# A two-layer recurrent decoder step on one Trainium2 core: side work handed out per half chunk in pieces, sample states by a block-diagonal operand, other first loads and another last root

## The chip, the cores and the metric

The kernel runs on one core of a Trainium2 chip. A core has TensorE (PE, matrix products), VectorE (DVE), ScalarE (ACT) and GpSimd (POOL); SyncE (SP) here only issues DMA transfers. The metric is the device time of one execution in microseconds. The time before is the median of three runs; the predicted time is set beside that median.

## The reference, cut to what matters

All in fp32: a prompt of 256 tokens and 8 samples of 8 tokens each, 320 columns together, pass through two layers. Every layer is one large input projection, three recurrent branches, their projections, gates and an output projection.

```python
def _layer(x, pos0, ...):
    xn = _rmsnorm(x, lp['norm_g'])                      # x: (tokens, 2048)
    proj = xn @ lp['w_in']                              # u, z of three branches; q, k, v; three gates
    ...
    y_s5 = ...                                          # diagonal complex recurrence, GELU, GLU
    y_lru = ...                                         # gated linear recurrence after a conv of 4
    y_ret, n_ret = _retention(q, k, v, r_ret, pos0, lp['ret_gn_g'])
    b_s5 = (y_s5 * silu(z_s5)) @ lp['w_branch_s5']
    b_lru = (y_lru * silu(z_lru)) @ lp['w_branch_lru']
    b_ret = (y_ret * silu(z_ret)) @ lp['w_branch_ret']
    merged = sigmoid(g_s5) * b_s5 + sigmoid(g_lru) * b_lru + sigmoid(g_ret) * b_ret
    return x + merged @ lp['w_out'], ...
def _retention(...):                                    # 8 heads, 128 x 128 states
    r_new = r * g_chunk + einsum('bjhd,bjhe->bhde', kc * zeta, vc)
...
y = _rmsnorm(x, final_norm_g)                           # after the second layer
```

For the samples the line `r_new` gives 8 states of 128x128 for every head, each from 8 tokens. All new states are outputs too.

## The kernel before, in words

All weights pass through one stream. A chunk is 512 KB of weights (4 k-tiles of 128 rows, 256 columns); 624 chunks come by DMA on SP's queue into `raw` (4 buffers), in an order written out in `blocks`. Each chunk is used in two half chunks, 1248 in all. For a half chunk ACT writes a rounded copy `whi` of the weights (`copy`, line 126) and DVE the rest `wlo` = raw − whi (`sub`, line 99), both 128x512; then PE runs 12 main matmuls with 320 columns: 2 column halves n, 2 k-tiles kk, 3 passes (lines 1321 to 1323: hi·xh, hi·xl, lo·xh). The activations are split in the same way (`xh`, `xl`; `yhl` for a branch; `GH`; `M`). `whi` and `wlo` share a pool of 4 buffers (`phl`), so that the copy for half chunk u waits for PE's line 1322 of half chunk u−4. They are emitted `lead` half chunks ahead of their use: 3 at most places, up to 8 in chunks 25 to 64, where a tile `more` gives five further buffers.

All other work (the recurrences, gates, norms and states) is side work: Python generators that emit a piece, `yield`, and are resumed by `step`. `stream` calls `step` once after each chunk; `yield n` holds a generator back n chunks. `step` lets a generator wait when the modelled load of DVE or ACT is over `BEHIND`, which is 99 and so never. The emitted order is the order on every engine: a side piece between two half chunks stands between two `wlo` on DVE. Results of side matmuls go to four PSUM buffers `ps`, in turn: a matmul that writes a buffer waits for whatever read the buffer's last content.

Retention, the side work that the change rewrites, runs for head pairs m = 0 to 3 of each layer. `ret_qk` turns q and k (`ra` = `ra` + `rsw`, line 99, 128x640); `ret_heads` multiplies them (line 894, `ps<-ra`), masks the scores (`rsc`, `scs`), transposes keys, and normalizes the result into the gate `z` (`z<-ps,pv,z`) which becomes `yhl`; `ret_state` makes the states. For the samples' states it multiplies values with a 0/1 mask per sample, so that one 128x512 matmul gives four samples (`rvm<-rkv,sm`, two of 128x512 on DVE, then two matmuls at line 1029, then `r<-r,ps`): 64 such muls and 64 such matmuls in all. A recurrence of S5 runs as a long chain of 128x64 operations on POOL (lines 563 to 566) beside retention.

At the start, `constants` and `more_constants` issue pv, ident, sm, pmask and the second pv on ACT's queue, and `x_load(0)` and the first chunk (two halves) on SP's, in turn. At the end, `finish` takes the inverse root of the summed squares: DVE adds eps, ACT takes Ln and Exp (one table load between them), DVE does one Newton step (`rstd`, three operations), and then 8 tiles `y` of two 128x320 halves are multiplied, 14 halves on DVE and 2 on POOL, each stored by a DMA when both its halves are done.

Of the kernel before, what the change touches and what calls it, by code (L numbers as in the profile page):

```python
# [24 lines left out]
SLOT, BEHIND = 3.26, 99  # L25
# [15 lines left out]
K_ZP, K_ZS, K_GP, K_G2, K_MC, K_VM = 0, 16, 24, 48, 72, 74  # L41
NK = 82


def shape_constants():
# [27 lines left out]
    for t in range(2):  # L73
        sm[:, K_MC + t] = ((p // 16) % 2 == t)
    for b in range(NB):
        sm[:, K_VM + b] = (p % 64 // NS == b)
# [4 lines left out]
class Program:  # L81
    def __init__(self, nc, tc, I, O, gamma8):
# [3 lines left out]
        self.load = dict(dve=0.0, act=0.0)  # L86
        self.table = None
# [6 lines left out]
    def dve(self, o, rate=1.04):  # L94
        self.load['dve'] += 0.065 + rate * 1e-3 * math.prod(o.shape[1:])
# [25 lines left out]
    def act(self, o, a, f, **k):  # L121
        self.load['act'] += 0.08 + 0.92e-3 * math.prod(o.shape[1:])
# [14 lines left out]
    def spawn(self, g, late=0):  # L137
        e = [g, 0, late]
        self.gens.append(e)
        self.gens.sort(key=lambda e: e[2])  # L140
        return e

    def step(self):
        for k in self.load:
            self.load[k] = max(0.0, self.load[k] - SLOT)
        for e in list(self.gens):
# [3 lines left out]
            if max(self.load.values()) > BEHIND:  # L150
                continue
            self.advance(e)

    def advance(self, e):
        try:
            r = next(e[0])
            e[1] = (r or 1) - 1
        except StopIteration:
            self.gens.remove(e)

# [15 lines left out]

    def exp_vec(self, out, x, t):
# [7 lines left out]
        yield  # L185
# [3 lines left out]
        yield  # L189
# [3 lines left out]
        yield  # L193

    def rsqrt_vec(self, out, v, t):
# [3 lines left out]
        for _ in range(3):  # L199
            self.mul(t, out, out)  # L200
            self.stt(t, t, -0.5, v, OP.mult, OP.mult)
            self.stt(out, t, 1.5, out, OP.add, OP.mult)


    def constants(self):
# [4 lines left out]
        nc.scalar.dma_start(self.pv[0], I['pv'][0])  # L210
# [3 lines left out]
        nc.vector.memset(self.fv, 1.0)  # L214

    def more_constants(self):
        nc, I = self.nc, self.I
        self.table_of(AF.Ln)
# [3 lines left out]
        nc.scalar.dma_start(self.ident, I['c_ident'])  # L222
        nc.scalar.dma_start(self.sm, I['c_sm'])
        nc.scalar.dma_start(self.pmask, I['c_pair'])
        for l in range(1, DEPTH):
            nc.scalar.dma_start(self.pv[l], I['pv'][l])
# [66 lines left out]
    def x_group(self, q):  # L293

        for c in range(4):
# [7 lines left out]
            if c % 2:  # L303
# [20 lines left out]
    def s5_setup(self, l):  # L324
        nc, I = self.nc, self.I
        t = self.rt([128, 32, 32], name="s5t")
# [21 lines left out]
        yield  # L348
# [10 lines left out]
        self.stt(h, n, -c3, h, OP.mult, OP.add)  # L359
        self.ts(h, h, 0.5, OP.mult)  # L360
        self.mul(z, h, h)
        yield
# [1077 lines left out]
```

## Time and profile before

| what | value |
|---|---|
| median of three runs (lowest, highest) | 2404.8 us (2404.71, 2404.82) |
| profiled execution, own time | 2406.62 us |
| profiled execution, span | 2404.8 us |
| PE busy | 2360.1 us, 98% |
| DVE busy | 1572.1 us, 65% |
| ACT busy | 1070.8 us, 45% |
| POOL busy | 605.9 us, 25% |
| DMA moved | 413.71 MB, mean 172 GB/s |
| mean granted TensorE clock | 0.995 of full speed |

Busy times are sums over the span. PE is the engine to look at: each microsecond in which it has nothing to do, or runs at its lower clock, is a microsecond of the kernel's time, and the other engines matter where PE waits for them.

### The profile page before, as it was taken

How to read it: one execution, taken by the hardware profiler on the slowest of the kernel's cores; microseconds unless marked ns; L12 is line 12 of the kernel's file. 1: busy time of each engine (PE TensorE's matmuls, PEld its weight loads, DVE VectorE, ACT ScalarE, POOL GpSimd, SP SyncE). 2: the span in 40 equal slices, each digit the busy share in tenths (PEclk: the TensorE clock that was granted, in tenths of full speed). 3: DMA queues.
4: the chain of work that ended last, by engine and by line, in shares of the span. 5: the costliest groups of instructions: out<-in, count | busy, mean ns of one | idle time of the engine just before them, and what ended most of it. 6: DMA issues, size and time to landing. Idle time of an engine off the chain costs nothing.

```text
span 2404.8 us, 44311 instructions
## 1 busy us (share of the span) xinstructions
PE 2360.1 (98%) x16746; PEld 2326.9 (97%) x16746; DVE 1572.1 (65%) x2900; ACT 1070.8 (45%) x1941; POOL 605.9 (25%) x1157
## 2 busy tenths in 40 slices
PE   8999999999999999999999999999999999999997
PEld 8999999889999999999999999999999999999997
DVE  7889466876774756755567665767776656555544
ACT  6655344333343434444555554433333334444443
POOL 2004001999920000300100000699950200000011
PEclk9999999999999999999999999999999999999998
DMA  6655587454654545446656587454555554444553
GB/s 213 220 173 166 159 218 211 126 172 159 193 171 164 168 151 173 152 151 195 201 165 190 162 223 206 147 182 137 168 170 168 178 184 157 149 153 146 158 179 118
DMA packets 153590, 413.71 MB, mean 172 GB/s; under 512 B 18592, under 2 KB 59296, under 8 KB 153120
## 3 DMA queue, kind: packets, MB, share of 16 engines
q1 hardware_dynamic: 152656, 410.58, 54.1%
q8 instruction: 131, 2.15, 0.4%
q14 instruction: 83, 0.68, 0.1%
q10 hardware_dynamic: 720, 0.30, 0.0%
HBM read 373.83 MB, written 31.74 MB: 169 GB/s over the span
## 4 chain that ended last, share of the span: by engine, by line
PE 95%; DVE 3%; DMA 1%; issue 0%; ACT 0%; SPq 0%; ACTq 0%; DVEq 0%
PE pt L1321 30%; PE pt L1323 29%; PE pt L1322 29%; DMA raw<-w_in 1%; PE ps L638 1%; PE ps L757 1%; DVE wlo L99 1%; DVE rvm L99 1%; PE ps L546 1%; PE ps L1029 1%; PE ps L894 0%; PE ps L953 0%; ACT whi L126 0%; DVE yt L99 0%; PE ps L1004 0%
## 5 line engine op out<-in xcount | busy, mean ns | idle before, releaser
L99 DVE TENSOR_TENSOR wlo<-raw,whi 128x512 fp32r<-128x512 f32 x1187 | 845.5, 727 | 758.1 <-ACT whi L126 737.4
L126 ACT ACTIVATE whi<-raw 128x512 fp32r<-128x512 f32 x1187 | 737.7, 629 | 1071.3 <-PE pt L1322 894.2
L1321 PE MATMUL pt<-xh,whi 128*128 128x320 f32 x3320 | 1037.5, 313 | 6.1 <-ACT whi L126 6.1
L1323 PE MATMUL pt<-xh,wlo 128*128 128x320 f32 x3320 | 1029.8, 310 | 7.6 <-DVE wlo L99 7.5
L1322 PE MATMUL pt<-xl,whi 128*128 128x320 f32 x3320 | 1027.6, 310 | 0.0
L1321 PEld LDWEIGHTS pt<-xh,whi 128*128 128x128 f32 x3320 | 625.6, 188 | 11.8 <-ACT whi L126 6.4
L1323 PEld LDWEIGHTS pt<-xh,wlo 128*128 128x128 f32 x3320 | 625.0, 188 | 11.5 <-DVE wlo L99 11.3
L1322 PEld LDWEIGHTS pt<-xl,whi 128*128 128x128 f32 x3320 | 625.4, 188 | 2.8
L1321 PE MATMUL pt<-yhl,whi 128*128 128x320 f32 x756 | 234.7, 310 | 0.0
L1323 PE MATMUL pt<-yhl,wlo 128*128 128x320 f32 x756 | 233.6, 309 | 0.0
L1322 PE MATMUL pt<-yhl,whi 128*128 128x320 f32 x756 | 233.6, 309 | 0.0
L563 POOL TENSOR_TENSOR cs<-H,l2r 128x64 f32<-128x64 f32 x254 | 121.2, 477 | 255.6 <-DVE H L113 235.9
L252 POOL TENSOR_TENSOR acc<-acc,sq 128x320 f32<-128x320 f32 x28 | 25.6, 914 | 586.4 <-ACT sq L126 585.4
L1321 PE MATMUL pt<-M,whi 128*128 128x320 f32 x512 | 158.7, 310 | 0.0
L1323 PE MATMUL pt<-M,wlo 128*128 128x320 f32 x512 | 158.2, 309 | 0.0
L1322 PE MATMUL pt<-M,whi 128*128 128x320 f32 x512 | 158.2, 309 | 0.0
L1321 PEld LDWEIGHTS pt<-yhl,whi 128*128 128x128 f32 x756 | 141.9, 188 | 0.8 <-issue 0.5
L1322 PEld LDWEIGHTS pt<-yhl,whi 128*128 128x128 f32 x756 | 141.9, 188 | 0.0
L1323 PEld LDWEIGHTS pt<-yhl,wlo 128*128 128x128 f32 x756 | 141.9, 188 | 0.0
L565 POOL TENSOR_TENSOR cs<-cs,H 128x64 f32<-128x64 f32 x254 | 132.3, 521 | 0.0
L564 POOL TENSOR_TENSOR cs<-H,l2i 128x64 f32<-128x64 f32 x254 | 123.8, 487 | 0.0
L566 POOL TENSOR_TENSOR H<-cs,cs 128x64 f32<-128x64 f32 x254 | 117.7, 463 | 19.9
(251 smaller groups left out, 2526.5 us busy)
## 6 DMA issues: line engine op xcount, KB each, us to landing
raw<-w_in SPq DMA_DIRECT2D x447, 512.0 KB, 4.4
raw<-w_out SPq DMA_DIRECT2D x64, 512.0 KB, 4.5
raw<-wb_lru SPq DMA_DIRECT2D x32, 512.0 KB, 4.7
raw<-wb_ret SPq DMA_DIRECT2D x32, 512.0 KB, 3.8
raw<-wb_s SPq DMA_DIRECT2D x32, 512.0 KB, 3.6
r<-sret SPq DMA_DIRECT2D x16, 512.0 KB, 8.0
ret_s<-r SPq DMA_DIRECT2D x16, 512.0 KB, 3.0
raw<-w_glu SPq DMA_DIRECT2D x16, 512.0 KB, 3.6
```

Source lines behind the costliest of these rows:

```text
L99: self.nc.vector.tensor_tensor(o, a, b, op=op)
L126: self.nc.scalar.activation(o, a, f, **k)
L252: self.nc.gpsimd.tensor_tensor(self.acc, self.acc, sq, op=OP.add)
L546: self.nc.tensor.matmul(pp[g][:, a * HN:(a + 1) * HN], wst[:, a, g * 128:(g + 1) * 128], ust[:, 2 * a + g], start=True, stop=True, skip_gr ...
L563: g.tensor_tensor(t1, old, lr, op=OP.mult)
L564: g.tensor_tensor(t2, self.swap(old), li, op=OP.mult)
L565: g.tensor_tensor(t1, t1, new, op=OP.add)
L566: g.tensor_tensor(new, t1, t2, op=OP.add)
L638: nc.tensor.matmul(o[q * 32:(q + 1) * 32], w[:, c, m], H[:, q0 + m, c, col:col + HN], start=col == 1 and c == 0, stop=c == 1, tile_positio ...
L1321: nc.tensor.matmul(o, hi[:, kk, cs], xh, start=k == 0, stop=False)
L1322: nc.tensor.matmul(o, hi[:, kk, cs], xl, start=False, stop=False)
L1323: nc.tensor.matmul(o, lo[:, kk, cs], xh, start=False, stop=k == nk - 1)
```

## The change

1. **Handing out.** `step` is called after each half chunk. `yield` holds a generator for two half steps (the chunk of before), the new `yield 0` splits a piece: the generator goes on at once unless it is `paced` and the modelled load is over `BEHIND` = 2.4 us; each half step takes `SLOT` = 1.8 us off that load. Long pieces (`exp_vec`, `s5_setup`, `lru_*`, `ret_heads`, ...) get many `yield 0`. `need` forces steps until a flag of the operand that a main matmul is about to read is set. The deep stretch ends at chunk 58 instead of 68, and side work of the setups starts earlier.
2. **Sample states.** The masks, `rkv` and `rvm` go. Keys and values of the samples are spread fourfold over 256 columns (`parts_of`, 32 ACT copies 128x256), transposed (`rows_of`, 64 transposes 128x128, while 16 transposes of line 918 go), and made hi or lo by partition (`rk4`, `rv4`: 16 ACT copies and 16 DVE operations of 128x512, and 16 `rkz` of 128x256 in place of 128x128). Four ACT copies per head (64 in all) write the values on the blocks of `vbd`, a tile that is zero elsewhere, and two matmuls 128x512 per head (32 in all) give the states.
3. **Start.** x comes in two 128x320 parts, pv and one 128x640 on ACT's queue; the first chunk in four parts on SP's; ident, sm, pmask and the second pv go to SP's queue after chunk 8. Eight matmuls ones·ones of 128x128 run first. The first half chunk is split per k-tile and its matmuls run in the order (n, kk) = (0,0), (1,0), (0,1), (1,1).
4. **Last root.** ACT's `Abs_reciprocal_sqrt` reads the sum directly, beside DVE's eps step; one Newton step; the result `rp` is a PSUM tile, and a copy `rs` in SBUF serves POOL, which multiplies 4 halves instead of 2.

```diff
-SLOT, BEHIND = 3.26, 99
+SLOT, BEHIND = 1.8, 2.4
...
-    def step(self):
+    def step(self, force=False):
         for k in self.load:
             self.load[k] = max(0.0, self.load[k] - SLOT)
         for e in list(self.gens):
             if e[1] > 0:
                 e[1] -= 1
                 continue
-            if max(self.load.values()) > BEHIND:
-                continue
-            self.advance(e)
+            while force or not (e[3] and e[4]) or max(self.load.values()) <= BEHIND:
+                if not self.advance(e):
+                    break
 
     def advance(self, e):
+
         try:
             r = next(e[0])
-            e[1] = (r or 1) - 1
         except StopIteration:
             self.gens.remove(e)
+            return False
+        r = 1 if r is None else r
+        e[1], e[4] = max(0, 2 * r - 1), r == 0
+        return r == 0
+
+    def need(self, *flag):
+        for _ in range(400):
+            if self.flag.get(flag):
+                return
+            self.step(force=True)
...
     def rsqrt_of(self, p):
+
         r = self.pl.tile([128, T], F32, name="rstd", tag="rstd")
-        for _ in self.rsqrt_steps(p, r):
-            pass
-        return r
+        v, t, q = (self.vt([128, T]) for _ in range(3))
+        rp = self.ps()[:, :T]
+        self.act(q, p[:, :T], AF.Abs_reciprocal_sqrt, scale=1.0 / D, bias=self.fv[:, 2, 0:1])
+        self.ts(v, p[:, :T], 1.0 / D, OP.mult, EPS, OP.add)
+        self.mul(t, q, q)
+        self.stt(t, t, -0.5, v, OP.mult, OP.mult)
+        self.stt(rp, t, 1.5, q, OP.add, OP.mult)
+        return r, rp
...
+    def rows_of(self, a):
+        p = self.ps()
+        for n in range(2):
+            for c in range(2):
+                q = slice(c * 128, (c + 1) * 128)
+                self.nc.tensor.transpose(p[:, n * 256 + c * 128:n * 256 + (c + 1) * 128], a[:, n, q], self.ident)
+        return p
...
         for n in range(2):
-            h, x = 2 * m + n, kv[n]
-            for s in range(2):
-                t = self.rt([128, 2, 4, 128], F32R, name="rvm")
-                mask = sm[:, K_VM + 4 * s:K_VM + 4 * s + 4][:, :, None].to_broadcast([128, 4, 128])
-                for i in range(2):
-                    self.mul(t[:, i], x[:, 1 + i][:, None, :].bitcast(F32).to_broadcast([128, 4, 128]), mask)
+            h = 2 * m + n
+            for b in range(4):
+                r = slice(32 * b, 32 * b + 32)
+                self.copy(self.vbd[r, :, b], v4[r, n].bitcast(F32))
+            yield
+            for c in range(2):
+                p = self.ps()
+                nc.tensor.matmul(p, k4[:, n, c * 128:(c + 1) * 128], self.vbd[:, c].rearrange("p b e -> p (b e)"),
+                                 start=True, stop=True)
                 yield
-                p = self.ps()
-                for i in range(2):
-                    nc.tensor.matmul(p, x[:, 0], t[:, i].rearrange("p b e -> p (b e)"), start=i == 0, stop=i == 1)
-                yield
-                rr = r0[n][:, 4 * s:4 * s + 4].rearrange("p b e -> p (b e)")
+                rr = r0[n][:, 4 * c:4 * c + 4].rearrange("p b e -> p (b e)")
                 self.stt(rr, rr, self.g8[h], p, OP.mult, OP.add)
...
-                elif j > 4 and n:
-                    nc.gpsimd.tensor_tensor(y[:, n], y[:, n], r, op=OP.mult)
+                elif j > 2 and n:
+                    nc.gpsimd.tensor_tensor(y[:, n], y[:, n], rs, op=OP.mult)
...
-        deep = (27, 2 * 68)
+        deep = (27, 2 * 58)
```

Three places show what moves. First DVE in retention of layer 0, head pair m = 1, in the kernel before: the work between one chunk's `wlo` pair and the next. `cb1`, `cb2` and `H` are a step of S5 (its input states), `r0` the sample state, `rv` the values.

```order
L99 TENSOR_TENSOR wlo_6414<-raw_6353,whi_6413 128x512
L99 TENSOR_TENSOR cb1_6429<-H_3036,l2r_2399 128x256
L99 TENSOR_TENSOR cb2_6430<-H_3036,l2i_2400 128x256
L99 TENSOR_TENSOR cb1_6429<-cb1_6429,cb2_6430 128x256
L99 TENSOR_TENSOR H_3036<-H_3036,cb1_6429 128x32x8
L99 TENSOR_TENSOR rsw_6392<-rsw_6392,ropr_4415 128x640
L99 TENSOR_TENSOR wlo_6442<-raw_6353,whi_6441 128x512
L99 TENSOR_TENSOR wlo_6458<-raw_6395,whi_6457 128x512
L119 SCALAR_TENSOR_TENSOR r0_5911<-r0_5911,ps_6435 128x512
L99 TENSOR_TENSOR rvm_6474<-rkv_6104,sm_126 128x512 x2
L99 TENSOR_TENSOR ra_6338<-ra_6338,rsw_6392 128x640
L99 TENSOR_TENSOR wlo_6482<-raw_6395,whi_6481 128x512
```

The same place in the changed kernel, m = 1; `rv4` and `rk4` stand elsewhere, `rvm` nowhere, and a piece stands after each half chunk.

```order
L98 TENSOR_TENSOR wlo_6520<-raw_6428,whi_6519 128x512
L98 TENSOR_TENSOR wlo_6553<-raw_6477,whi_6552 128x512
L98 TENSOR_TENSOR rv_6568<-pt_6343,rstd_693 128x640
L118 SCALAR_TENSOR_TENSOR r0_5980<-r0_5980,ps_6514 128x512
L98 TENSOR_TENSOR wlo_6576<-raw_6477,whi_6575 128x512
L118 SCALAR_TENSOR_TENSOR z_5998<-ps_6535,pv0_114,z_5998 128x256
L118 SCALAR_TENSOR_TENSOR z_5998<-ps_6535,pv0_114,z_5998 128x64
L98 TENSOR_TENSOR scs_5304<-ps_6550,rdms_6450 64x4x16
L98 TENSOR_TENSOR wlo_6595<-raw_6516,whi_6594 128x512
```

Where four or five operations stood between one `wlo` and the next, at most three stand here, and behind `wlo_6553` stand `rv_6568` and then `r0_5980`, the reader of `ps_6514`; behind `wlo_6576` stand the two `z_5998`, the readers of `ps_6535`.

PE at that place in the changed kernel. The first row is the last main matmul of a half chunk, whose weights are `whi_6454` and `wlo_6455`; line 1076 transposes, lines 970, 971 and 974 are the score products (894, 895 and 898 before).

```order
L1425 MATMUL pt_6518<-xh_158,wlo_6455 128x320
L1076 MATMUL ps_6535<-ident_603,ron_6333 128x128 x3
L970 MATMUL ps_6544<-ra_6199,ra_6378 128x256
L971 MATMUL ps_6544<-ra_6199,ra_6378 128x128
L970 MATMUL ps_6547<-ra_6199,ra_6378 128x256
L971 MATMUL ps_6547<-ra_6199,ra_6378 128x128
L974 MATMUL ps_6550<-ra_6199,rkd_6539 128x128
L1423 MATMUL pt_6518<-xh_164,whi_6479 128x320
```

`ps_6550` is in the buffer of `ps_6514`, so line 974 waits for `r0_5980` above. `wlo_6553`, which stands ahead of that on DVE, is the part of a half chunk four further on: `whi_6552` and `wlo_6553` take the buffers of `whi_6454` and `wlo_6455`, which PE leaves only at the first row. Twelve main matmuls later line 1108 writes `ps_6571`, in the buffer of `ps_6535`, so it waits for the two `z_5998`, which stand behind `wlo_6576`; that one takes the buffers of the half chunk which PE has just finished. No side matmul of the kernel before stands this close to a reader behind such a `wlo`, apart from those that wait for a rotated key or query.

Last, DVE at the very end, before and then in the changed kernel (`ps` in the last three rows is `rp`).

```order
L99 TENSOR_TENSOR sq<-yt 128x320
L115 TENSOR_SCALAR vt<-ps 128x320
L99 TENSOR_TENSOR vt<-rstd 128x320
L119 SCALAR_TENSOR_TENSOR vt<-vt 128x320
L119 SCALAR_TENSOR_TENSOR rstd<-vt,rstd 128x320
L99 TENSOR_TENSOR yt<-yt,rstd 128x320 x6
L119 SCALAR_TENSOR_TENSOR yt<-yt,pv_112,rstd 128x320 x2
L99 TENSOR_TENSOR yt<-yt,rstd 128x320 x6
```

```order
L98 TENSOR_TENSOR sq<-yt 128x320
L114 TENSOR_SCALAR vt<-ps 128x320
L98 TENSOR_TENSOR vt<-vt 128x320
L118 SCALAR_TENSOR_TENSOR vt<-vt 128x320
L118 SCALAR_TENSOR_TENSOR ps<-vt 128x320
L98 TENSOR_TENSOR yt<-yt,ps 128x320 x6
L118 SCALAR_TENSOR_TENSOR yt<-yt,pv_115,ps 128x320 x2
L98 TENSOR_TENSOR yt<-yt,ps 128x320 x4
```

Two halves move from DVE to POOL, and Newton's last operation and its readers go from an SBUF tile to PSUM.

## Rows read from the trace of the kernel before

**Rows 1.** The page: busy time by engine, and the chain that ended last.

```profile
PE 2360.1 (98%) x16746; PEld 2326.9 (97%) x16746; DVE 1572.1 (65%) x2900; ACT 1070.8 (45%) x1941; POOL 605.9 (25%) x1157
PE 95%; DVE 3%; DMA 1%; issue 0%; ACT 0%; SPq 0%; ACTq 0%; DVEq 0%
```

**Rows 2.** Windows: length, busy PE, PEld, DVE, ACT, POOL; PEclk, DMA share, GB/s.

```profile
0.00:60.00 60.00, 53.88 (x346) 53.50 (x347) 43.91 (x97) 36.74 (x69) 13.02 (x18) 1.00 0.63 214
...
420.00:480.00 60.00, 55.38 (x387) 52.73 (x387) 51.32 (x111) 21.03 (x44) 55.46 (x117) 0.97 0.41 127
...
840.00:900.00 60.00, 60.00 (x411) 60.00 (x410) 31.05 (x45) 23.39 (x37) 0.00 (x0) 1.00 0.46 151
...
2160.00:2404.00 244.00, 228.28 (x1550) 227.10 (x1548) 120.83 (x180) 102.72 (x171) 13.58 (x15) 0.97 0.47 151
sum 2404.00, PE 2360.13 PEld 2326.89 DVE 1572.13 ACT 1070.80 POOL 605.86; mean PE 90.77 PEld 89.50 DVE 60.47 ACT 41.18 POOL 23.30
```

**Rows 3.** Waits: engine, line and releaser: us in total, times, longest.

```profile
ACT whi L126 <- PE pt L1322: 894.2, 784, 8.1
...
PEld ps L894 <- DVE ra L99: 12.0, 6, 2.9
...
PEld pt L1323 <- DVE wlo L99: 11.3, 15, 3.2
...
PEld ps L1029 <- DVE rvm L99: 3.9, 8, 0.6
...
PEld ps L1029 <- PE pt L1323: 3.1, 6, 0.7
```

**Rows 4.** Chain around 495 and 525 us: start, us, what.

```profile
492.43 0.82 DVE rvm L99
...
495.99 0.46 PE ps L1029 x2
...
525.38 0.89 PE ps L1004 x8
```

**Rows 5.** DVE groups, 420 to 660 us: count, busy, mean ns, idle before.

```profile
L99 DVE TENSOR_TENSOR wlo<-raw,whi 128x512 fp32r<-128x512 f32 x106 | 80.6, 784 | 46.2 <-ACT whi L126 43.1 <-PE ps L870 2.9
...
L119 DVE SCALAR_TENSOR_TENSOR r<-r,ps 128x512 f32<-128x512 f32 x12 | 8.1, 677 | 0.0
...
L119 DVE SCALAR_TENSOR_TENSOR z<-ps,pv,z 128x256 f32<-128x256 f32 x6 | 2.8, 472 | 0.0
...
L99 DVE TENSOR_TENSOR rv<-pt,rstd 128x640 f32<-128x640 f32 x3 | 2.4, 811 | 0.0
```

**Rows 6.** DVE groups, 840 to 960 us.

```profile
L99 DVE TENSOR_TENSOR wlo<-raw,whi 128x512 fp32r<-128x512 f32 x68 | 46.8, 691 | 45.8 <-ACT whi L126 45.3
L99 DVE TENSOR_TENSOR g<-pt,rstd 128x640 f32<-128x640 f32 x5 | 4.1, 817 | 0.0
```

**Rows 7.** ACT group, 420 to 700 us.

```profile
L126 ACT ACTIVATE whi<-raw 128x512 fp32r<-128x512 f32 x127 | 79.2, 630 | 157.9 <-PE pt L1322 109.9 <-DMA raw<-w_in 23.1 <-issue 15.3
```

**Rows 8.** Timeline of the start: start, us, engine, what [idle before, releaser].

```profile
4.53 1.01 ACT L126 ACTIVATE xh<-xin,pv 128x320 fp32r<-128x320 f32 x2 [1.87 <-DMA pv<-pv]
...
6.12 0.64 PE L1321 MATMUL pt<-xh,whi 128*128 128x320 f32 x1 [6.12 <-ACT whi L126]
...
12.08 0.33 PE L1321 MATMUL pt<-xh,whi 128*128 128x320 f32 x1
```

**Rows 9.** Timeline of the end.

```profile
2388.94 0.49 DVE L115 TENSOR_SCALAR vt<-ps 128x320 f32<-128x320 f32 x1 [1.08 <-PE ps L1100]
...
2390.01 1.28 ACT L126 ACT_TABLE_LOAD   x1
...
2393.45 3.83 DVE L99 TENSOR_TENSOR yt<-yt,rstd 128x320 f32<-128x320 f32 x6
2393.59 2.13 POOL L1117 TENSOR_TENSOR yt<-yt,rstd 128x320 f32<-128x320 f32 x2 [14.99 <-DVE rstd L119]
2395.04 6.13 SPq L1120 DMA_DIRECT2D y<-yt  x8
2398.13 2.49 DVE L99 TENSOR_TENSOR yt<-yt,rstd 128x320 f32<-128x320 f32 x6
```

More of the change, by code (lines that the diff above doesn't have):

```diff
@@ L72, in shape_constants @@
             sm[:, K_G2 + 3 * h + s] = v * v
[L73 to L76, printed above, removed]
+    sm[:, K_LO] = -1.0 * (p // 8 % 4 >= 2)
+    sm[:, K_LO + 1] = -1.0 * (p // 8 % 2)
     return dict(c_rope=rope, c_dm=dm.astype(f), c_dms=dms.astype(f), c_sm=sm.astype(f),
@@ L94, in dve @@
     def dve(self, o, rate=1.04):
-        self.load['dve'] += 0.065 + rate * 1e-3 * math.prod(o.shape[1:])
+        self.load['dve'] += (0.16 + rate * 1e-3 * math.prod(o.shape[1:])) * self.slow
     def tt(self, o, a, b, op):
@@ L214, in constants @@
         nc.vector.memset(self.fv, 1.0)
+        p = self.ps()
+        for _ in range(8):
+            nc.tensor.matmul(p[:, :128], self.ones, self.ones, start=True, stop=True)
     def more_constants(self):
         nc, I = self.nc, self.I
-        self.table_of(AF.Ln)
         self.ident = self.pc.tile([128, 128], F32, name="ident")
@@ L677, in s5_gelu_pair @@
         self.split(GH[:, 0, 2 * j:2 * j + 2], GH[:, 1, 2 * j:2 * j + 2], y)
+        while not self.flag.get(('z5', l, j)):
+            yield
+        yield 0
         self.mul(self.sz5[j], self.sz5[j], y)
-        self.flag['glu', j] = True
+        self.flag['glu', l, j] = True
     def s5_glu(self, l, j, pt):
@@ L739, in lru_u @@
         xc, r, i = [], [], []
+        while j and not self.flag.get(('y', l, 0, j - 1)):
+            yield
         for n in range(2):
@@ L1130, in xn, with yb, y, gh @@
                 return (self.xl if kind else self.xh)[k]
-            def yb(kind, k):
-                return self.yhl[k // 2][:, kind, k % 2]
+            def yb(br, l=l):
+                def y(kind, k):
+                    self.need('y', l, br, k // 2)
+                    return self.yhl[k // 2][:, kind, k % 2]
+                return y
+            def gh(kind, k, l=l):
+                self.need('glu', l, k // 2)
+                return self.GH[:, kind, k]
+            def mm(kind, k, l=l):
+                self.need('M', l, k // 2)
+                return self.M[:, kind, k]
             def inp(col, fn, *a):
@@ L1274, in stream @@
         self.constants()
-        for _ in zip(self.x_load(0), load(0, 2)):
-            pass
-        self.more_constants()
+        x0 = self.x_load(0)
+        next(x0)
+        nc.scalar.dma_start(self.pv[0], self.I['pv'][0])
+        list(x0)
+        list(load(0, 4))
+        self.table_of(AF.Ln)
         x = [self.x_load(q) for q in range(1, 4)]
@@ L1283, in stream @@
         self.norm_begin()
-        group = self.x_group(0)
-        next(group)
-        prep(0)
+        group = self.x_group(0, 1)
+        hi = self.phl.tile([128, 2, 256], F32R, name="whi", tag="whi")
+        lo = self.phl.tile([128, 2, 256], F32R, name="wlo", tag="wlo")
+        for k in range(2):
+            next(group)
+            self.split(hi[:, k], lo[:, k], raw[0][:, k])
+        hl[0] = hi, lo
         next(group)
         prep(1)
+        list(group)
         prep(2)
```

269 lines of the change are left out of this document (162 added, 107 removed).

## The prediction

> **What bounds the kernel now.** I read the page first: PE is busy for 98% of the span, and the chain that ended last is PE for 95% of its length [rows 1]. So the kernel lasts as long as its matmuls, and what can be won is the time in which PE has nothing to do or runs at its lower clock. The windows say where that is [rows 2]: in all PE is idle for 2404.0 − 2360.1 = 43.9 us, of which 6.1 us lie before the first matmul, 15.7 us in the last window, where the output is scaled and stored, and the other 22.0 us in between. There they lie in the stage in which DVE is close to full and POOL runs its chain (PE 55.4 of 60 us with DVE at 51.3 and POOL at 55.5); with DVE at 31.0 and POOL idle PE is busy for all of 60 us. So mid-stream the limit is not how much DVE does in the whole run (65%) but how late a single DVE result comes.
>
> The table of waits names the results [rows 3]. PE's weight loads wait 12.0 us for rotated keys and queries (line 894), 11.3 us for `wlo`, 3.9 us for `rvm` and 3.1 us more at line 1029, which belong to the same pairs of masked operands. Together 30.3 us; this is more than the 22.0 us of idle PE, since the matmul ahead of a late load still drains and the next one starts from nothing, and the matmuls' starts slip by the longer figure. ACT, on the other hand, waits 894 us for PE in front of `whi` [rows 3]: it has slack, and the weights are ready ahead where DVE is not behind. One of the waits in detail [rows 4]: the chain runs through `rvm` on DVE, then the rotation, then PE. The reader is to see that a burst on DVE between two `wlo` holds up whatever comes behind it.
>
> The spells of low clock are the third loss: PEclk is 0.97 in that window of 420 to 480 us and in two others of that kind. 0.03 of 60 us is 1.8 us, but part of each spell is also a wait; I put them at 2.0 us in all.
>
> **The middle.** What goes: 64 `rvm` of about 0.8 us each leave DVE [rows 4], against 16 operations of the same shape and a few more columns in `rkz`, so some 35 us net; and pieces are cut, so that no long burst stands between two `wlo`. In before's order seven places of 4.8 us and one of 6.2 us of side work (by row means) stand between two `wlo`; after, none has over 2.8 us. A matmul takes 60 us / 411 = 0.146 us [rows 2], a half chunk of twelve 1.75 us and three half chunks of lead 5.3 us, so a burst of 2.8 us with a `wlo` of 0.78 us behind it [rows 5] fits in the lead. The rotated key stands a half chunk or two ahead of the matmul that reads it. I take the old waits off but for 2.5 us: −30.3 − 2.0 + 2.5 = −29.8 us.
>
> What comes: waits that the new order forces. Line 974 at half chunk 249 of layer 0 waits for a chain that starts only when PE ends the half chunk before it: `whi` 0.63 us [rows 7], `wlo` 0.78, `rv` 0.81, `r` 0.68 [rows 5], 2.9 us. PE meanwhile has three transposes and four score products, about 1.0 us at 0.11 us per 128x128 [rows 4], so it waits 1.9 us. The next, line 1108 for the two `z`, has whi 0.63 + wlo 0.78 + z 0.47 and an estimated 0.25 for its short part: 2.1 us less the last main matmul, 2.0 us. For m = 2 and 3 line 1108 stands behind the `z` product of 0.81 us: 2.2 us less about 1.0 us of side matmuls, 1.25 us each. That is 6.4 us in a layer, 12.8 us in two. Only in layer 0, two more: at half chunk 115 a gate matmul of the recurrent branch waits behind a `wlo`, a gate product, ACT's `whi` and sigmoid and two copies (3.1 us); at 131 the main matmul of the branch waits for `yhl`, forced there by `need`, behind a `wlo`, four `z` products and both parts of `yhl` (3.4 us). Both are sums of the same rows and estimates of the like. In all 19.3 us. Queued behind them is only PE itself, whose wait passes on at once. The four of 1.9 us and the two of over 3 may bring spells of low clock, as before's longer waits seem to: 2.0 us, bounds 0 and 6. A wait could also be shorter, since `whi` may be started by the last reads one matmul earlier: bounds 12 and 22 us.
>
> PE's own work: 32 matmuls of 0.23 us and 16 transposes of 0.11 us go, 64 of 0.11 us come [rows 4]: −7.4 − 1.8 + 7.0 = −2.2 us; a switch between side and main matmuls is a few hundredths of a microsecond and there are more of them, 1.4 us: −0.8 us. ACT takes some 64 + 32 + 16 copies more, by the nearest row (0.63 us for 512 columns [rows 7]) 35 to 45 us, less the 48 small ones that go; its cover is the 894 us of waiting. If that cover is gone where a `whi` stands behind four of them, `wlo` is late next, by 1 us a place.
>
> So the middle: −29.8 + 19.3 + 2.0 − 0.8 = −9.3 us.
>
> **The start.** PE first waits for `whi`, which stands behind the two `xh`, which wait for pv; pv is the last thing that ACT waits for [rows 8]. Parts of x of half the size come first, `whi` of 256 columns is some 0.3 us shorter than one of 512, and only one `xh` of 0.5 us stands ahead of it: first matmul 0.75 us earlier, at 5.35. The first matmuls run at half clock, until 12.08 us [rows 8]. PE had been busy for 6.0 us then. If the clock follows PE's work, a start 0.75 us earlier and eight matmuls ahead of it bring the rise forward; I take half of the 6.0 us, and 3 us at half clock cost 1.5 us. It is bounded by the weights, as the chunks after the first land no earlier than before. −2.3 us; bounds −0.5 and −3. The constants on SP's queue after chunk 8 pass some 0.3 MB ahead of a chunk that is three chunks early: nothing, or 0.7 us.
>
> **The end.** PE ends at 2388.9; the muls start at 2393.45 [rows 9]. The chain to them loses one DVE step that becomes parallel, and Ln with the table load (1.28 us): what is left is an ACT operation of 0.5 us and three of DVE's of 0.5 us, so 2391.1, 2.35 us sooner. Then the muls. Before, the first six on DVE take 3.83 us beside POOL's two of 1.07 us, the last six alone 2.49 us [rows 9], 0.42 each. After, DVE has 12 of them with `rp` in PSUM. `wlo` with two SBUF operands takes 784 ns beside the chain and 691 without [rows 5, 6], while a product with a PSUM operand takes 811 and 817 ns [rows 5, 6]: so PSUM operands spare DVE the slowing, and 12 × 0.45 = 5.4 us end at 2396.5, POOL's four at 2391.75 + 4 × 1.07 = 2396.0. Stores went out from 2395.04 before, spaced by what the queues move; with the first one 3.0 us sooner and the last 4 us sooner, the end is 3.7 us sooner. If DVE is slowed all the same: −1.8 us.
>
> The Trainium skill, "SBUF — State Buffer", section "SBUF: two separate sides", says that DVE with two SBUF inputs and GpSimd reading SBUF share a port pair as an exclusive lock, the later one waiting for the whole instruction. By it a product with one SBUF operand is free, as in the rows; were each wait a whole instruction, the six products before would have lost about two POOL operations, 2.1 us, and 3.83 − 2.49 = 1.34 us is what they lost. The measured figure decides.
>
> **The sum.** −9.3 − 2.3 − 3.7 = −15.3 us. The profiled execution has a span of 2404.8 us and an own time of 2406.6; the sum is made on the span, which equals the median of the runs. 2404.8 − 15.3 = 2389.5 us; I say 2390.
>
> **The rivals.** (a) The forced waits don't cost: ACT or DVE get through before PE arrives, because PE is late by itself at these places, or the chain starts from an earlier buffer. For it: ACT's slack [rows 3]. Against it: the buffers of `whi` bind by the order, whatever the slack. Then 2390 − 19.3 − 2.0 = 2369 us. (b) The change doesn't do what it says: the bursts go, but the keys are late by the rotation's own length (the 12.0 us at line 894 stay), with the forced waits on top, and the end gives 1.8 us. −15.3 + 12.0 + 1.9 = −1.4 us: 2403 us, no measurable difference; a measurement of this kernel can tell about 0.2%, 4.8 us, from none. For it: the rotation contains a transfer (`rsw`), whose landing the change doesn't move. Against it: its chain in the trace ran through `rvm` [rows 4]. (c) Slower: side matmuls stand after every half chunk now, so the four `ps` buffers turn over at a `wlo` which PE itself has just released, in far more than the ten places counted. Price 1.25 us each; from 16 places more, 15.3 + 4.8 = 20.1 us, the kernel is slower: 2410 us. For it: ten such places are there already. Against it: elsewhere the readers stand two or more half chunks ahead.
>
> A rule that bears on (a): "TensorE: Matmul & The Clock Gate", Part 2 ("What happens when you issue a matmul") of the Trainium skill, says that only weight loads are pulled ahead and matmuls stay in program order. By that rule a main matmul cannot pass a waiting side matmul. The rows agree, with loads waiting 12.0 us and nothing run past them [rows 3].
>
> **Chances and range.** Forecast (2376 to 2399) 0.62, (a) 0.22, (b) 0.11, (c) 0.05. The range leaves out half of (a) below and most of (b) and (c) above: 2369 to 2401 us. Faster by over 0.2%: 0.62 + 0.22 and a little of (b)'s lower end, 0.85; within 0.2% 0.10; slower 0.05.
>
> **What would show it.** Right: at about 450 to 620 us and in the same stage of layer 1, waits of PE at lines 974 and 1108 for DVE's `r0` and `z` of 1 to 2 us, some 13 us in all, no `wlo` row of PE over 4 us, and lines 970 (894 before) under 3 us; a first matmul near 5.4 us; muls from 2.35 us after the sum. Wrong: these waits absent (a), line 970 still at 10 us (b), many short waits at `ps` (c), `rp` products of over 0.6 us beside POOL.

## The result and the profile after

| | before | after |
|---|---|---|
| median (lowest, highest) | 2404.76 us (2404.29, 2404.82) | 2423.72 us (2419.41, 2425.49) |
| ratio | 1 | 1.0077 [1.0059, 1.0094] |
| span of the profiled execution | 2404.8 us | 2423.7 us |
| mean granted clock | 0.995 | 0.988 |

The change makes the kernel 0.77% slower, 18.9 us by the spans, where it was forecast to be some 15 us faster. The busy times of the page after, to be held against [rows 1]:

```profile
PE 2369.4 (98%) x16778; PEld 2340.4 (97%) x16778; DVE 1533.1 (63%) x2830; ACT 1107.3 (46%) x2019; POOL 588.4 (24%) x1159
```

DVE has 39 us less to do and ACT 36 us more, about as forecast. But PE is idle for 2423.7 − 2369.4 = 54.3 us. Before its first main matmul it stands for 1.5 us and behind its last one for 13.9 us, both less than before; between them it stands for 38.9 us, where it was 22.0. The windows after (columns as in [rows 2]) show where:

```profile
0.00:60.00 60.00, 57.07 (x362) 54.63 (x363) 43.34 (x98) 37.12 (x70) 14.43 (x18) 1.00 0.67 231
...
240.00:300.00 60.00, 55.25 (x418) 53.38 (x418) 38.45 (x79) 31.46 (x63) 3.49 (x9) 0.94 0.73 200
480.00:540.00 60.00, 53.76 (x381) 52.35 (x380) 33.02 (x58) 22.48 (x48) 54.80 (x134) 0.94 0.46 153
540.00:600.00 60.00, 56.91 (x373) 56.19 (x372) 40.06 (x85) 25.65 (x54) 55.01 (x126) 0.94 0.54 178
600.00:660.00 60.00, 56.45 (x395) 55.46 (x394) 39.52 (x85) 24.21 (x50) 21.04 (x48) 0.94 0.44 142
...
1740.00:1800.00 60.00, 56.85 (x371) 56.13 (x370) 38.69 (x73) 26.18 (x55) 37.47 (x85) 0.94 0.52 172
```

The start is better than in [rows 2]. Retention (480 to 660 us, and 1680 to 1860 in layer 1) and the end of the recurrent branch (240 to 300) lose, although DVE is at 33 to 40 of 60 us there. PEclk of 0.94 says that every one of these windows holds matmuls at half clock. In the trace 121 main matmuls start some 0.27 us behind the one ahead of them instead of 0.15, which is 14.5 us; before it was 35, of which 18 at the start.

PE's waits, from the table of waits after (columns as in [rows 3]):

```profile
PE ps L974 <- DVE r L118: 13.7, 6, 3.9
PE ps L1108 <- DVE z L118: 6.7, 4, 2.2
PE ps L1108 <- DVE scs L98: 3.8, 2, 1.9
...
PE pt L1423 <- ACT yhl L125: 2.7, 1, 2.7
PE ps L804 <- DVE k L98: 2.4, 1, 2.4
PE ps L581 <- issue: 1.7, 1, 1.7
PE ps L804 <- DVE lxc L118: 1.5, 1, 1.5
...
PE ps L970 <- DVE ra L98: 0.9, 2, 0.5
```

The first three rows, with 24.2 us at lines 974 and 1108, are the waits in retention that the prediction named and put at 12.8 us. Of the old waits, PE's for rotated keys are down from 10.4 to 0.9 us (12.0 to 1.4 by its weight loads, as [rows 3] counts) and those for `rvm` are gone. The first of these places in the timeline after:

```profile
492.63 0.31 PE L1425 MATMUL pt<-xh,wlo 128*128 128x320 f32 x1
...
496.16 0.63 ACT L125 ACTIVATE whi<-raw 128x512 fp32r<-128x512 f32 x1 [1.58 <-DMA raw<-w_in]
...
496.83 0.87 DVE L98 TENSOR_TENSOR wlo<-raw,whi 128x512 fp32r<-128x512 f32 x1 [2.44 <-ACT whi L125]
...
497.62 0.81 DVE L98 TENSOR_TENSOR rv<-pt,rstd 128x640 f32<-128x640 f32 x1
...
498.35 0.67 DVE L118 SCALAR_TENSOR_TENSOR r<-r,ps 128x512 f32<-128x512 f32 x1
...
499.17 0.46 PE L974 MATMUL ps<-ra,rkd 128*128 128x128 f32 x2 [3.91 <-DVE r L118]
```

The chain is the forecast's, operation by operation and size by size: `whi`, `wlo`, `rv`, `r`, then PE. Its head differs. `whi` was to start when PE leaves the buffer, which is at 492.9 us, the end of the first row; here ACT waits for a DMA, its weights, and starts 3.2 us after that. Those weights were issued late. SP's waits after show what held its queue, with the two rows of before that answer to them in the second fence:

```profile
SPq L890 <- ACT rraw L125: 47.0, 10, 7.2
SPq L890 <- PE ps L1076: 45.2, 6, 10.4
```

```profile
SPq L840 <- ACT rraw L126: 11.3, 4, 4.8
...
SPq L840 <- ACT whi L126: 1.7, 5, 0.5
```

Line 890 (840 before) issues the transfer of a rotated tile `rsw` and stands on SP's queue ahead of weight loads. After the change it waits 6 times, up to 10.4 us, for PE's line 1076: the tile takes the buffer of `ron`, which the transposes of `z` still have to read. Six is also the count of waits at line 974.

Late loads as such are not new. ACT's waits for weights from 420 to 700 us, which hold retention of layer 0, before and then after:

```profile
ACT whi L126 <- DMA raw<-w_in: 23.1, 8, 4.7
```

```profile
ACT whi L125 <- DMA raw<-w_in: 22.7, 9, 3.9
```

They are as long before the change. New is the side matmul that waits for a reader behind the `wlo` of such a load.

### The profile page after: what moved, and what is told of

Same layout as the page of the kernel before. It is cut to its first block, busy times and chain, and to the rows that moved or that the text cites. A ratio compares the mean times of both kernels' runs of the same rounds, so it can differ in the third digit from the quotient of the medians.

```text
span 2423.7 us, 44413 instructions
## 1 busy us (share of the span) xinstructions
PE 2369.4 (98%) x16778; PEld 2340.4 (97%) x16778; DVE 1533.1 (63%) x2830; ACT 1107.3 (46%) x2019; POOL 588.4 (24%) x1159
## 5 line engine op out<-in xcount | busy, mean ns | idle before, releaser
L98 DVE TENSOR_TENSOR wlo<-raw,whi 128x512 fp32r<-128x512 f32 (+1 forms) x1199 | 854.3, 721 | 800.7 <-ACT whi L125 789.8
L125 ACT ACTIVATE whi<-raw 128x512 fp32r<-128x512 f32 (+1 forms) x1199 | 745.8, 629 | 1070.0 <-PE pt L1424 923.0
L1423 PE MATMUL pt<-xh,whi 128*128 128x320 f32 x3352 | 1053.9, 314 | 1.4 <-ACT whi L125 0.9
L1424 PE MATMUL pt<-xl,whi 128*128 128x320 f32 x3352 | 1042.2, 311 | 0.8 <-DVE xl L118 0.8
L1425 PE MATMUL pt<-xh,wlo 128*128 128x320 f32 x3352 | 1042.3, 311 | 0.2 <-DVE wlo L98 0.2
L1423 PEld LDWEIGHTS pt<-xh,whi 128*128 128x128 f32 x3352 | 635.6, 190 | 7.0 <-issue 4.1
L1424 PEld LDWEIGHTS pt<-xl,whi 128*128 128x128 f32 x3352 | 635.4, 190 | 4.8 <-DVE xl L118 1.5
L1425 PEld LDWEIGHTS pt<-xh,wlo 128*128 128x128 f32 x3352 | 634.8, 189 | 0.9 <-DVE wlo L98 0.7
L1423 PE MATMUL pt<-yhl,whi 128*128 128x320 f32 x768 | 239.3, 312 | 2.7 <-ACT yhl L125 2.7
L1424 PE MATMUL pt<-yhl,whi 128*128 128x320 f32 x768 | 238.1, 310 | 0.2 <-DVE yhl L98 0.2
L600 POOL TENSOR_TENSOR cs<-cs,H 128x64 f32<-128x64 f32 x254 | 118.1, 465 | 0.0
```

Source lines behind the costliest of these rows:

```text
L98: self.nc.vector.tensor_tensor(o, a, b, op=op)
L125: self.nc.scalar.activation(o, a, f, **k)
L600: g.tensor_tensor(t1, t1, new, op=OP.add)
L1423: nc.tensor.matmul(o, hi[:, kk, cs], xh, start=k == 0, stop=False)
L1424: nc.tensor.matmul(o, hi[:, kk, cs], xl, start=False, stop=False)
L1425: nc.tensor.matmul(o, lo[:, kk, cs], xh, start=False, stop=k == nk - 1)
```

## The experiments

The runs before, beside which each was timed, had medians of 2404.8 to 2407.5 us.

**Start and end alone**, in the kernel before (first loads, warm-up matmuls, split of the first half chunk, last root).

> The kernel before with the new start and the new last root alone; handing out and sample states as before. Both theories for the middle expect the same here: the start gives 2.0 us and the end 2.7 us, as the changed kernel's trace shows against before's, so about 2400.1 us. If the start's gain depended on the earlier side work, or the end's on the new states, it would stay near 2403 us or over.

Measured: 2403.29 us, ratio 0.9989 [0.998, 0.9998]. The time behind PE's last matmul falls from 16.00 to 13.29 us, so the end gives 2.7 us; at 215 us the matmuls are 1.2 us ahead. The middle has its old waits (9.9 us at the rotated keys' line). Right in direction, and smaller than forecast; the loss is not here.

**The old handing out** in the changed kernel: a step per chunk, no pacing.

```diff
-SLOT, BEHIND = 1.8, 2.4
+SLOT, BEHIND = 3.26, 99
-        e[1], e[4] = max(0, 2 * r - 1), r == 0
+        e[1], e[4] = max(0, r - 1), r == 0
...
                 if h:
...
-                self.step()
+                    self.step()
```

> The changed kernel with side work handed out once per chunk and without pacing; new states, start and end stay. Theory P (side matmuls wait for a PSUM buffer whose reader stands on DVE behind a wlo of the half chunk that PE has just finished): the readers stand one half chunk nearer, so PE's waits at lines 974 and 1108 fall from 25 to under 6 us, and what returns is bursts on DVE without rvm, some 8 us: 2385 to 2400 us, 2394 likeliest. Theory S (SP's queue is held by the rsw transfers and the ret_s stores, and late weight loads make the waits): the tiles and transfers are the same, so the waits stay: over 2410 us. Theory L (the new states themselves cost PE and ACT time): over 2412 us.

Measured: 2503.9 us, ratio 1.0405 [1.0389, 1.0421]. A miss: it doesn't undo the change, since by the code all pieces that are joined by `yield 0` now come as one burst. From its waits:

```profile
PE pt L1425 <- DVE wlo L98: 26.6, 7, 17.0
```

PE waits 17.0 us for one `wlo`. The waits at 974 and 1108 fall to 1.0 us or less each, but this run says nothing on the forecast's terms.

**Readers half a step later.** In the changed kernel 13 `yield` behind a side matmul become `yield 0.5`, so that the reader of its result is handed out one half step later instead of two.

```diff
             nc.tensor.matmul(p, k4[:, n, c * 128:(c + 1) * 128], self.vbd[:, c].rearrange("p b e -> p (b e)"),
                              start=True, stop=True)
-            yield
+            yield 0.5
             rr = r0[n][:, 4 * c:4 * c + 4].rearrange("p b e -> p (b e)")
```

> The changed kernel, in which the reader of a side PSUM tile is handed out one half step after its matmul, not two. Nothing else changes. Theory P: the reader no longer stands behind such a wlo in retention, and in the first branch of layer 0 it stands nearer; waits at lines 974 and 1108 (25 us) nearly gone, 5 to 9 us less at lines 804 and 581, and 8 to 12 us of low clock less: 2380 to 2392 us, 2387 likeliest. Theory S: loads land late as before, PE then waits for wlo or whi by 2 to 4 us at six places: over 2405 us. Theory L: over 2412 us.

Measured: 2375.81 us, ratio 0.987 [0.9854, 0.9887], 48 us under the changed kernel. Its windows in retention:

```profile
480.00:540.00 60.00, 60.00 (x444) 59.34 (x443) 45.41 (x95) 29.07 (x60) 55.30 (x121) 1.00 0.55 174
540.00:600.00 60.00, 59.21 (x435) 58.07 (x434) 41.40 (x88) 27.43 (x57) 55.22 (x122) 1.00 0.58 175
```

No wait at 974 or 1108 is left and no spell of half clock, with the same work on every engine. Of the 49.6 us between the spans, PE's idle time makes 28.9 (54.3 against 2374.1 − 2348.7 = 25.4) and half clock 14.5; 6.2 us aren't assigned.

**The same in retention alone** (9 of the 13).

> The changed kernel, with readers half a step later only in retention (nine yields in ret_qk, ret_state, ret_heads); the first branch's and the pooled yields stay. Theory A (the loss is the retention's waits at lines 974 and 1108, their 25 us, and the low clock that follows them): retention gives back 33 to 42 of the 48 us that the half step gave everywhere, total 2382 to 2391, and the waits at lines 804, 581 and for yhl in the first 300 us stay. Rival B (half or more of the loss comes from the first branch's waits and what follows them): total 2395 to 2405.

Measured: 2386.56 us, ratio 0.9927 [0.991, 0.9943]. Retention gives back 37 of the 48 us; the other 11 lie outside it, where the waits at 804, 581 and for `yhl` stay as they were (8.7 us in all) and half clock follows them.

**The score of line 974 in another PSUM tile** (the free columns of the score tile before it), so that it takes no buffer of its own.

```diff
-        p = self.ps()
-        nc.tensor.matmul(p[:, :128], kd.rearrange("p n t -> p (n t)"), q[:, :, SEQ:], start=True, stop=True)
+        p = pp[0][:, 384:]
+        nc.tensor.matmul(p, kd.rearrange("p n t -> p (n t)"), q[:, :, SEQ:], start=True, stop=True, skip_group_check=True)
```

> The changed kernel, in which the samples' score product (line 974) goes into the free 128 columns of the first score tile, so that this piece takes two PSUM buffers and not three. Theory P: the 13.7 us of waits at line 974 for r0 vanish with one spell of low clock per layer or more; line 1108 then waits for r0 in place of z, by 1 to 2 us each as now: 2405 to 2411 us, 2408 likeliest. Theory S: no change within 3 us of 2422. Theory L: no change.

Measured: 2399.84 us, ratio 0.9968 [0.9957, 0.9979], more than expected.

```profile
PE ps L1108 <- DVE r L118: 9.8, 6, 2.1
```

The waits at 974 are gone and the next writer of a `ps` waits for the same `r`, 9.8 us in place of 24.2; half clock falls from 14.5 to 4.7 us.

**`rsw` and `ret_s` on POOL's queue** instead of SP's, to let the weights pass.

```diff
-        nc.sync.dma_start(sw[0:64], raw[64:128])
-        nc.sync.dma_start(sw[64:128], raw[0:64])
+        nc.gpsimd.dma_start(sw[0:64], raw[64:128])
+        nc.gpsimd.dma_start(sw[64:128], raw[0:64])
...
-            nc.sync.dma_start(O['ret_s'][l, h], r0[n])
+            nc.gpsimd.dma_start(O['ret_s'][l, h], r0[n])
```

> The changed kernel, in which the rsw transfers and the ret_s stores are issued on POOL's queue, so that SP's queue holds no weight load behind them; the readers of side PSUM tiles stay where they are. If late loads lengthen the waits at lines 974 and 1108 (in the changed kernel's trace the whi of that chain starts 0.1 us after its load lands), the 25 us fall to 10 to 14 us with half of the low clock: 2400 to 2410 us. If the readers' place alone makes the waits, nothing changes: 2418 us or more. POOL's chain is held at times; it has over 100 us until its result is read, so this should cost nothing.

Measured: 2701.28 us, ratio 1.1224 [1.1207, 1.124]. Failed as a repair: the transfers now stand among POOL's chain of S5, and PE waits once per layer for a `wlo`, 159.7 and 131.7 us.

```profile
PE pt L1425 <- DVE wlo L98: 293.2, 3, 159.7
POOL rsw L890 <- ACT whi L125: 137.9, 6, 25.5
...
PE ps L974 <- DVE r L118: 5.9, 6, 2.0
```

The last row is of use all the same: where the loads have landed, line 974 waits at most 2.0 us, near the forecast's 1.9, instead of 3.9.

**A buffer of its own for `rsw`**, the clean form of that test. The instructions stand in the same order on PE, DVE, ACT and POOL; `rsw` leaves the pool `pw`, which gets 9 buffers instead of 10, so that its other tiles take their turns otherwise too.

```diff
-        sw = self.wt([128, 2, T], name="rsw")
+        sw = self.pl.tile([128, 2, T], F32, name="rsw", tag="rsw")
...
-            self.pw = pool("pw", 10)
+            self.pw = pool("pw", 9)
```

> The changed kernel with its instructions in the same order on every engine; only the rotated keys' and queries' tile rsw has a buffer of its own (and the pool that it came from has 9 buffers instead of 10), so SP's queue no longer stands at line 890 for a buffer that PE still reads, and the weight loads behind it go out earlier. Theory A (late loads make the chains to line 974 longer than the forecast's sum): line 974 at the first place of each layer waits 2.0 us instead of 3.9, the retention's waits fall from 24.2 us to 13 to 17, fewer low-clock spells follow, total 2404 to 2414. Rival B (the loads are late for another reason, or the chains are long by themselves): waits at 974 and 1108 stay within 3 us of 24.2, total 2420 to 2427.

Measured: 2400.87 us, ratio 0.9984 [0.9975, 0.9994]: 22.9 us under the changed kernel, beyond what theory A gave. ACT's waits for weights from 420 to 700 us fall from 22.7 us to one:

```profile
ACT whi L125 <- DMA raw<-w_in: 1.7, 1, 1.7
```

That one is at the first place, in its timeline here:

```profile
493.69 0.63 ACT L125 ACTIVATE whi<-raw 128x512 fp32r<-128x512 f32 x1 [1.69 <-DMA raw<-w_in]
494.35 0.69 DVE L98 TENSOR_TENSOR wlo<-raw,whi 128x512 fp32r<-128x512 f32 x1 [2.54 <-ACT whi L125]
494.96 0.82 DVE L98 TENSOR_TENSOR rv<-pt,rstd 128x640 f32<-128x640 f32 x1
495.70 0.68 DVE L118 SCALAR_TENSOR_TENSOR r<-r,ps 128x512 f32<-128x512 f32 x1
...
496.52 0.46 PE L974 MATMUL ps<-ra,rkd 128*128 128x128 f32 x2 [2.40 <-DVE r L118]
```

The eight places of retention that the forecast counted now wait 2.40, 2.06, 0.57 and 0.49 us in layer 0 and 3.05, 2.04, 0.61 and 0.49 in layer 1, 11.7 in all against the forecast's 12.8; line 974 of m = 2 and 3, which it had not counted, waits under 0.2 us each. At the first place of each layer `whi` still waits for its load, though for less long: it starts 1.2 and 1.9 us after PE has left the buffer instead of 3.2 and 3.5. So line 974 waits 2.40 and 3.05 us there and not theory A's 2.0. (SP's queue now stands at line 960, whose tile `rdm` comes from the same pool, 4 times and up to 5.7 us for PE's line 1076.) Half clock falls from 14.5 to 6.2 us.

**The masks of before for the sample states**, in the version with readers half a step later.

```diff
-            for b in range(4):
-                r = slice(32 * b, 32 * b + 32)
-                self.copy(self.vbd[r, :, b], v4[r, n].bitcast(F32))
...
+                t = self.rt([128, 2, 4, 128], F32R, name="rvm")
+                mask = sm[:, K_VM + 4 * s:K_VM + 4 * s + 4][:, :, None].to_broadcast([128, 4, 128])
+                for i in range(2):
+                    self.mul(t[:, i], x[:, 1 + i][:, None, :].bitcast(F32).to_broadcast([128, 4, 128]), mask)
...
+                for i in range(2):
+                    nc.tensor.matmul(p, x[:, 0], t[:, i].rearrange("p b e -> p (b e)"), start=i == 0, stop=i == 1)
```

> The half-step kernel with the samples' states of the kernel before (masks, rvm, two matmuls per four samples); handing out, half-step readers, start and end stay. If the rewritten states carry the gain in retention, DVE is near full there again and PE waits for rvm and wlo as before: 2384 to 2395 us. If the handing out alone carries it, 2376 to 2380 us: the matmuls that the masks need cost 2 us more on PE and nothing else.

Measured: 2394.57 us, ratio 0.995 [0.9935, 0.9965]. The page, a wait and a window of retention:

```profile
PE 2355.5 (98%) x16762; PEld 2327.6 (97%) x16762; DVE 1580.6 (66%) x2908; ACT 1077.4 (45%) x1939; POOL 613.8 (26%) x1159
```

```profile
PE ps L672 <- DMA yu<-du: 10.5, 3, 7.8
```

```profile
480.00:540.00 60.00, 60.00 (x443) 59.46 (x443) 43.90 (x94) 24.58 (x49) 55.14 (x124) 1.00 0.57 179
```

With the masks back, PE is still busy for all of retention (60.00 of 60 us in every window from 420 to 720 and from 1560 to 1860 us): the handing out, with the readers half a step later, takes the old waits off without the lighter DVE. The time falls into the range of the other theory, but not for its reason. The 18.8 us over the run without masks lie elsewhere: PE is busy 2355.5 − 2348.7 = 6.8 us longer (2.3 of them half clock) and idle 11.5 us longer, 10.5 of that at line 672 behind retention. As two scratch tiles also change their pool here, the cause of that wait is left open.

**`rp` in SBUF** instead of PSUM, in the version with readers half a step later.

```diff
-        rp = self.ps()[:, :T]
+        rp = self.vt([128, T])
```

> The half-step kernel with the last root in SBUF instead of PSUM. Its products on DVE then have two SBUF operands beside POOL's four: the first six take about 0.64 us each as in the kernel before, not 0.40, and each of POOL's over 1 us, not 0.87; the last store is 1.5 to 2.5 us later: 2377.3 to 2378.3 us. If the operand's place makes no difference: 2375.8 us, and the stores' own pace sets the end.

Measured: 2377.75 us, ratio 0.9879 [0.9862, 0.9895]. The time behind PE's last matmul grows from 13.29 to 15.45 us. Its end:

```profile
2363.05 5.15 DVE L98 TENSOR_TENSOR yt<-yt,vt 128x320 f32<-128x320 f32 x6
2363.60 4.26 POOL L1199 TENSOR_TENSOR yt<-yt,rstd 128x320 f32<-128x320 f32 x4 [13.56 <-ACT rstd L125]
```

Six products take 5.15 us beside POOL, 0.86 each; with `rp` in PSUM they follow each other by 0.42.

**Three repairs together**: readers half a step later, `l2r` and `l2i` computed ahead of POOL's products, setups begun later (`yield 16` and `6` for `10` and `4`).

> The half-step kernel (2375.8 us) with two more edits: in the S5 setup the five small DVE operations for l2r and l2i stand ahead of those that release POOL's products (in its trace they take 0.97 to 1.25 us each beside POOL, against 0.18 alone, and wlo behind them is 2.9 us late), and in layer 0 the S5 setups start 8 chunks later, away from the first branch (waits of 2.5 and 1.3 us for lxc). If both stalls come from those places: 2375.8 - 3.4 - 3.8 = 2368.6 us, 2367 to 2372. If DVE is simply full there, the second stays: 2372 us; if the late start of the setups brings a wait further on, over 2375 us.

Measured: 2371.5 us (2370.41 to 2371.9), ratio 0.9852 [0.9837, 0.9867], the best kernel of the study, 36 us under the kernel before. Its longest wait behind the first matmul is 0.96 us.

**That without the eight warm-up matmuls.**

> The version with readers half a step later, l2r and l2i ahead and earlier setup (2371.5 us), but without the eight ones-by-ones matmuls at the start. Theory A (these matmuls bring the clock's rise forward): main matmuls run at half clock until some 6 us after the first of them, as in the kernel before (6.12 to 12.08), that is to about 11 us instead of 6.2; the start loses 1.5 to 2.5 us, total 2373 to 2374. Rival B (the rise comes as early without them, or the weights bound the start): within 0.5 us of 2371.5.

Measured: 2372.09 us (2371.04 to 2373.72), ratio 0.9865 [0.985, 0.9879]: the medians don't tell it from the kernel with them. The two profiles do, with the first row at full clock here and then with the warm-up:

```profile
10.43 0.33 PE L1421 MATMUL pt<-xl,whi 128*128 128x320 f32 x1 
```

```profile
9.33 0.30 PE L1424 MATMUL pt<-xl,whi 128*128 128x320 f32 x1
```

The rise is 1.1 us earlier with the warm-up. In the changed kernel's own profile, with the same start, it came by 6.17 us, so that one profile of each can't price these matmuls.

**That with a buffer of its own for `rsw`.**

> The same buffer in the version with readers half a step later, l2r and l2i ahead and earlier setup (2371.5 us). Theory A (a late load costs only where a side matmul waits for a wlo of that load): nothing, 2370 to 2373. Rival B (SP's holds cost time by themselves): 2 us or more off, under 2369.

Measured: 2371.85 us (2370.51 to 2371.95), ratio 0.986 [0.9845, 0.9874]. Nothing, as theory A has it: where no side matmul waits for a late reader, the hold on SP's queue costs nothing.

## Why the prediction was wrong

Forecast 2390 us, measured 2423.7: slower, where faster was forecast. The signs of the terms were right; the sizes of the new waits and of the low clock were not, and one queue was left out.

- **Old waits off (−29.8 us): right as far as the runs show.** The rotated keys' line waits 0.9 us; with the new waits removed the kernel comes to 2375.8 us, near the 2369 that rival (a) gave for that case. The reason given was half wrong: the masked products needed not leave DVE for it (run with the masks).
- **Forced waits in retention (12.8 us): the place and the chain right, the head of the chain wrong. This is the step that failed.** The prediction put it as a chain "that starts only when PE ends the half chunk before it". In the changed kernel it starts when a late weight load lands. After the change `rsw` falls on the buffer of `ron`, and SP's queue stands at line 890 until PE has read that. (The spread keys and values come from the same pool, and the order is another; which of the two shifts the turn wasn't tried.) The prediction counted no buffer of that pool and named no wait on SP's queue; of `rsw` it said that the change doesn't move its landing. It took the weights as ready ahead where DVE is not behind, although its own [rows 7] have ACT wait 23.1 us for loads in that stage. With a buffer for `rsw` the waits of the places counted are 11.7 us; without it those at lines 974 and 1108 are 24.2.

  That 11.7 comes close to the forecast's 12.8 is in part luck. PE's side work ahead of these waits was put at 1.0 us, with each score product counted once. In the trace each is two matmuls, as in the chain of before (columns as in [rows 4]):

  ```profile
  495.11 0.43 PE ps L894 x2
  495.55 0.22 PE ps L895 x2
  ```

  Two such pairs are 1.3 us, 1.6 with the three transposes. For m = 2 and 3 the four products and line 974 make 1.5. With these in place of 1.0 the prediction's own sums give 1.3 us for the first place and 0.7 for line 1108 of m = 2 and 3, where 0.49 to 0.62 were measured. At the first places the load that was still late made up for the difference.
- **Low clock (2.0 us, bounds 0 and 6): off by 12.5.** 14.5 us after, all but one matmul in spells that follow a wait of 1.3 us or more. With `rsw`'s buffer 6.2, a little over the upper bound. Of the 22.9 us that this buffer was worth, 12.5 are waits of retention and 8.3 half clock; 2.1 aren't assigned.
- **Forced waits in layer 0's first branch (6.5 us): nearly right.** 2.4 + 0.4 us at line 804, and 2.7 for `yhl` with 1.7 just ahead of it at line 581, a side matmul that the prediction didn't name; an unforeseen 1.5 at line 804 makes 8.7.
- **Bursts between two `wlo` ("none has over 2.8 us"): wrong at one place.** The row means of `l2r` and its like made them short; at 984 us they stand beside POOL's products and take 1.0 to 1.2 us each, and PE waits 2.9 us at the `wlo` behind them.
- **PE's work (−0.8 us): too small**, by the run with the masks 4.5 to 6.8 us.
- **Start (−2.3 us): −1.2, in the run of start and end alone.** In the changed kernel the first main matmul came at 5.30 us, as said, and full clock by 6.17, sooner than said; but PE then waits again, 0.4 us at 6.8 for `whi` and, which that run doesn't have, 0.8 at 28.9 for `xl`.
- **End (−3.7 us): −2.7.** The products didn't slow, as argued from the PSUM operand (0.42 us each), but begin 2.7 us behind the sum instead of the forecast 2.2, and then DVE stands 0.5 us for the copy of `rs`:

```profile
2409.07 1.34 PE L1182 MATMUL ps<-sq,ones 128*128 128x320 f32 x4 [0.55 <-ACT sq L125]
2410.51 0.53 ACT L125 ACTIVATE vt<-ps,fv 128x320 f32<-128x320 f32 x1 [1.49 <-PE ps L1182]
2411.14 0.49 DVE L114 TENSOR_SCALAR vt<-ps 128x320 f32<-128x320 f32 x1 [1.70 <-ACT vt L125]
...
2413.12 0.89 DVE L98 TENSOR_TENSOR yt<-yt,ps 128x320 f32<-128x320 f32 x2
...
2414.51 1.68 DVE L98 TENSOR_TENSOR yt<-yt,ps 128x320 f32<-128x320 f32 x4 [0.50 <-ACT rstd L125]
```

The eps step, forecast beside ACT's root, waits for it. Both read the sum's PSUM tile; that this is the reason wasn't tried.

With these sizes in place of the forecast's the sum would be −15.3 + 11.4 + 2.2 + 12.5 + 2.9 + 1.1 + 1.0 = +15.8 us, and 4 to 6 less by PE's work; measured are +18.9. The rest isn't assigned. As in the kernel before, matmul starts slip by more than PE's idle time shows (30.3 us against 22.0 there).

Of the rivals, (c) had the sign but not the reason: the places that cost are the ten named, line 974 of m = 2 and 3 and a few outside retention, not many short ones; most of them cost more, and the clock about as much again. The keys of (b) were not late.

## What to carry to other kernels

Where a matmul waits for a reader that stands behind an operation just released, follow that operation's input too. ACT waited for loads in retention before the change as long as after it; what made them cost was a side matmul behind them. With the readers handed out sooner ACT waits 28.2 us for loads from 420 to 700 us, and PE is idle for 0.8 us there. A change that takes tiles from a shared pool moves who waits for whose buffer, on DMA queues as well; list the waits of each queue before and after. And hand out the reader of a side result before the next buffer is needed: one half step was worth 48 us here.

## What the runs showed of the hardware

Small DVE operations beside POOL's, in the timeline after (128x32 elements; `l2r` takes 0.18 to 0.19 us in the best kernel, where it stands ahead of POOL's products):

```profile
984.51 1.05 DVE L98 TENSOR_TENSOR l2r<-lamr 128x32 f32<-128x32 f32 x1
985.49 0.18 DVE L98 TENSOR_TENSOR s5t<-lami 128x32 f32<-128x32 f32 x1
985.70 1.25 DVE L98 TENSOR_TENSOR l2r<-l2r,s5t 128x32 f32<-128x32 f32 x1
986.87 1.09 DVE L118 SCALAR_TENSOR_TENSOR l2i<-lamr,lami 128x32 f32<-128x32 f32 x1
```

POOL's operations there take 1.06 to 1.39 us. An operation of 0.2 us that meets one is held for about its whole length, so the price goes by POOL's operation and not by DVE's. The Trainium skill, "SBUF — State Buffer", section "SBUF: two separate sides", states an exclusive lock between DVE with two SBUF inputs and GpSimd reading SBUF, held for a whole instruction. These rows agree, and so do the products of the end, 0.86 us with `rp` in SBUF and 0.42 with it in PSUM.

The same start reached full clock by 6.17 us in one profiled execution (the changed kernel) and at 9.3 in another (the best kernel). The Trainium skill, "TensorE: Matmul & The Clock Gate", Part 1, says that the number of slow first matmuls differs from run to run of one kernel; these profiles agree.

The length of a wait of PE does not alone tell whether half clock follows. With `rsw`'s buffer a spell followed the wait of 3.05 us (layer 1) but not the one of 2.40 (layer 0); in the kernel before, one followed a wait of 2.0 us at 564 us, and none followed one of 2.6 us at 494 us.
